# A hybrid backbone layer: the output projection's last token tile and the first SwiGLU products in another order

## The chip, the cores and the metric

The program runs on one core of a Trainium2 chip. The metric is device time in microseconds (us). One execution was also taken by the hardware profiler; all rows below are from it.

## The reference, cut to what matters

One layer over 256 context and 1024 latent tokens of 1024 columns, in float32. A mixer (two groups of heads) gives `y`; after it come an output projection with a gated residual, a modulated RMSNorm, and SwiGLU with a gated residual:

```python
    x = x + g1 * (y[:, CTX_LEN:] @ w_out[layer])
    x = x + g2 * swiglu(modulate(rms_norm(x, norm_ffn_g[layer]), sh2, sc2),
                        w_ffn_in[layer], w_ffn_out[layer])
    return rms_norm(x, final_g)
```

`w_ffn_in` is 1024 x 5632, gate and up halves of 2816 columns each.

## The kernel before

Every float32 product is made of three TensorE passes over operands that were split into a high part (`hi`, the rounded value, written by ScalarE) and a low part (`lo`, the rest, a subtraction on VectorE or GpSimd): hi*hi, hi*lo, lo*hi.

**The projection (op).** The latent tokens are eight tiles of 128 (l = 0 to 7). `wo_half(n)` loads and splits one half (512 columns) of the projection's weights. For a tile, `op_y` turns and splits y, `op_mm(y, n)` makes one half of the output columns (24 matmuls of 128x512) and adds the residual on VectorE (L1139, L1140), and `op_norm` does the rest: it stores x1 to memory, squares it on ScalarE (L1148), takes the reciprocal root, scales the tile in two halves (L1150 VectorE, L1151 ScalarE), turns it in eight transposes (L1158, `x1T`), modulates it (`hf`), and makes the operands of the next stage. The tiles come in pairs, 0, 4, 1, 5, 2, 6, 3, 7, since the next stage is a Winograd-Strassen scheme over two halves of the tokens (tiles 0 to 3, tiles 4 to 7) and two halves of the 1024 inner columns.

**The first SwiGLU matrix (ffn).** The operands of the tokens are seven sets: b11 and b21 (the two halves of columns for tiles 0 to 3), b22, and the differences t1 to t4, each as hi and lo. Operand column l % 4 of a set comes from tile l or l - 4, so t1 to t4 and b22 are complete only after tile 7. For an output block f of 128 columns, `ffn_w` takes the weights raw from `wraw` or from a sum (`ws`, GpSimd, L1250) and splits them (`split`, L314 ScalarE and L315 VectorE); `product(f, i)` is one of seven products of 12 matmuls of 128x512; `combine` reads the bank. Products 1 (a11 x b11) and 2 (a12 x b21) fill the same PSUM bank, and `combine(f, 1)` copies it to `m1` between them (L1285). Products 5, 6, 7, 4 need t1, t2, t3, t4. The first two blocks (f = 0 and 11) are taken together, product by product, in the order 1, 2, 5, 6, 7, 4, 3; the others one at a time. `w_sums` makes sums of the second SwiGLU matrix's weights on GpSimd, in between.

**What sets the order.** The code is written in the order in which a scheduler takes it up; the scheduler may move an instruction ahead of others on its engine, and `tc.issue_after` ties one behind another. On the chip each engine works its list off in order and waits for semaphores. A pool's memory can be used anew once the last reader of what lay there is done: `FW` (raw SwiGLU weights and their splits) takes the place of `WO` (the projection's weights), which is closed after the last tile's second `op_mm`.

At the hand-over from op to ffn the code was:

```python
            op_mm(y, int(l == 7))
            if before:
                op_norm(*before)
            op_mm(y, int(l != 7))
            before = l, y
        close(WO)
        close(OY)
        FW = pool("fw", bufs=2)
...
        for f in (0, FT // 2):
            ffn_load(f)
        banks(**{"f%d" % i: 1 for i in range(8)})
        op_norm(*before, tr=("f3", "f7"))
```

Of the kernel before, what the change touches and what calls it, by code (L numbers as in the profile page):

```python
# [17 lines left out]
P = 128  # L18
# [19 lines left out]
def build(nc, tc, ap, dbg=None, stop=None, marks=None):  # L38
# [122 lines left out]
    try:  # L161
# [15 lines left out]
        ones = const("ones", [P, P])  # L177
# [276 lines left out]
        R2 = pool("r2", bufs=2)  # L454
        ada2 = C.tile([P, 2, KT], F32, tag="ada2", name="ada2")
# [628 lines left out]
        OY = pool("oy", bufs=2, side="right")  # L1084
        WO = pool("wo", side="right")
        S.dma_start(gain, ap["gains"])
        slabs = [X[n][:, i, 3].rearrange("p k t -> p (k t)") for n in X for i in range(2)]

        def wo_half(n):

            hi, lo, raws = [], [], [woraw[k % 2] for k in range(KT)]
            if n == 0:
                raws = [OP.tile([P, 4, P], F32, tag="hf", name="hf", bufs=4).rearrange("p k t -> p (k t)")
                        for _ in range(4)]
                for _ in range(2):
                    x1 = OP.tile([P, D], F32, tag="x1", name="x1", bufs=2)
                    raws += [x1[:, 0:512], x1[:, 512:1024]]
            for k in range(KT):
# [3 lines left out]
                for x, nm in ((hi, "hi"), (lo, "lo")):  # L1102
                    x.append(slabs.pop(0) if n and slabs else
                             WO.tile([P, 512], F32R, tag="wo%s%d%d" % (nm, n, k), name="wo" + nm, bufs=1))
# [9 lines left out]
        def op_y(l):  # L1114
            yhi = OY.tile([P, KT, P], F32R, tag="yhi", name="yhi")
            ylo = OY.tile([P, KT, P], F32R, tag="ylo", name="ylo")
            for half in range(2):
                yt = load(OY, dy[l, :, half * 512:half * 512 + 512], "yt", 3, (P, 512))
# [23 lines left out]
        held = {}  # L1142

        def op_norm(l, y, tr=("pc", "pc")):
# [7 lines left out]
            sl = slice((l % 4) * P, (l % 4 + 1) * P)  # L1152
            for half in range(2):
                pt = bank(tr[half], "x1T")
                hf = OP.tile([P, 4, P], F32, tag="hf", name="hf", bufs=4)
                for i in range(4):
                    k = half * 4 + i
                    T.transpose(pt[:, i * P:(i + 1) * P], x1[:, k * P:(k + 1) * P], ident)  # L1158
                for i in range(4):
                    k = half * 4 + i  # L1160
                    if l % 4 == 3 and i % 2:
# [5 lines left out]
                held[l // 4, half] = hf  # L1167
                e = V if l % 4 == 3 else G

                def part(n, src):  # L1170
# [3 lines left out]
                def diff(n, r, p, q, op=ALU.subtract):  # L1174
                    e.tensor_tensor(r, p, q, op)
                    part(n, r)
# [12 lines left out]

        before = None  # L1190
        pairs = (0, 4, 1, 5, 2, 6, 3, 7)
        nxt = op_y(0)
        for i, l in enumerate(pairs):
            y = nxt
            if l != 7:
                nxt = op_y(pairs[i + 1])
            op_mm(y, int(l == 7))
            if before:
                op_norm(*before)
            op_mm(y, int(l != 7))  # L1200
            before = l, y
        close(WO)
        close(OY)
        FW = pool("fw", bufs=2)
        raws = {}

        last_wfi = [None]
# [380 lines left out]
```

## Time and profile before

| what | value |
|---|---|
| median of 3 runs | 1484.49 us (1481.42 to 1485.3) |
| the profiled execution | 1489.96 us, span of its instructions 1488.2 us |
| granted TensorE clock, mean | 0.976 of full speed |
| TensorE busy | 1403.8 us, 94% of the span |
| projection, 728 to 835 us | TensorE busy 103.83 of 107 us |
| hand-over, 835 to 848 us | TensorE busy 7.45 of 13 us, clock 0.61 |
| first SwiGLU matrix after it, 848 to some 1300 us | TensorE busy nearly throughout |

Busy times of an engine are the sum of its instructions; TensorE's matmuls overlap, so in a dense stretch what counts is the distance from one start to the next. The profiled execution is 5.47 us above the median.

### The profile page before, as it was taken

Reading aid. Unit: us, or ns where it says so; the run is one execution under the profiler, and the core shown is the slowest. Engines: PE = TensorE matmul, PEld = TensorE weight load, DVE = VectorE, ACT = ScalarE, POOL = GpSimd, SP = SyncE. Lnnn points to the kernel's source line nnn. Section 1 sums busy time; section 2 is a strip of 40 time slices with the busy share of each in tenths; the row PEclk is TensorE's granted clock in tenths of the full one; section 3 lists DMA queues with packets and bytes.
Section 4 is the critical chain, followed back from the end, with each engine's and each line's share of the span. In section 5 each row is a group of like instructions: output and inputs, shape, how many; then the busy total and the mean of one; then the engine's idle time right before and its main releaser. Section 6 shows DMA issues by size and latency. Waiting matters only on the chain.

```text
span 1488.2 us, 24210 instructions
## 1 busy us (share of the span) xinstructions
PE 1403.8 (94%) x8919; PEld 1206.0 (81%) x8919; DVE 970.4 (65%) x1934; ACT 606.0 (41%) x1268; POOL 639.4 (43%) x589
## 2 busy tenths in 40 slices
PE   7999999987889999999799899999999999999997
PEld 1898888976878889998688688877888888788886
DVE  6566788378868335778767787656555555657477
ACT  5543564375451111244544433323333333444444
POOL 0120011476124333234326579999555553335321
PEclk9999999997989999999999899999999999999999
DMA  9536686478687745995643256665222232785863
GB/s 324 206 114 203 185 261 200 155 248 252 190 243 199 263 157 203 377 378 202 229 148 110 90 186 231 252 237 198 106 107 107 106 142 74 235 290 184 303 209 114
DMA packets 173751, 298.16 MB, mean 200 GB/s; under 512 B 43368, under 2 KB 93752, under 8 KB 168256
## 3 DMA queue, kind: packets, MB, share of 16 engines
q1 hardware_dynamic: 121760, 252.12, 49.5%
q10 hardware_dynamic: 49072, 35.83, 7.8%
q0 software_dynamic: 2800, 8.65, 1.6%
q8 instruction: 70, 1.15, 0.3%
q14 instruction: 49, 0.40, 0.1%
HBM read 206.60 MB, written 89.96 MB: 199 GB/s over the span
## 4 chain that ended last, share of the span: by engine, by line
PE 46%; DMA 9%; POOL 7%; DVE 4%; issue 3%; ACT 1%; SPq 1%; ACTq 0%; POOLq 0%; DVEq 0%
PE ffn L1279 6%; PE ffn L1277 6%; PE ffn L1278 6%; PE fo L1405 4%; PE fo L1403 4%; PE fo L1404 4%; DMA wd<-tw 2%; PE op L1136 2%; PE op L1138 2%; PE op L1137 2%; PE Tr L884 1%; DMA U<-xd 1%; POOL ws L1250 1%; PE tm L343 1%; POOL tw L1331 1%
## 5 line engine op out<-in xcount | busy, mean ns | idle before, releaser
L341 PE MATMUL tm<-whi,hhi 128*128 128x256 f32 (+1 forms) x704 | 201.0, 289 | 3.5 <-ACT xa L354 1.9
L342 PE MATMUL tm<-wlo,hhi 128*128 128x256 f32 (+1 forms) x704 | 201.9, 288 | 2.1 <-DVE wlo L315 2.1
L343 PE MATMUL tm<-whi,hlo 128*128 128x256 f32 (+1 forms) x704 | 199.8, 287 | 0.0
L341 PEld LDWEIGHTS tm<-whi,hhi 128*128 128x128 f32 x704 | 134.3, 192 | 7.3 <-ACT xa L354 2.5
L1277 PE MATMUL ffn<-t,whi 128*128 128x512 f32 x352 | 137.0, 390 | 1.4 <-ACT whi L314 1.4
L1279 PE MATMUL ffn<-t,wlo 128*128 128x512 f32 x352 | 137.1, 390 | 1.2 <-DVE wlo L315 1.2
L342 PEld LDWEIGHTS tm<-wlo,hhi 128*128 128x128 f32 x704 | 135.2, 192 | 3.4 <-DVE wlo L315 2.7
L1278 PE MATMUL ffn<-t,whi 128*128 128x512 f32 x352 | 137.0, 389 | 0.0
L343 PEld LDWEIGHTS tm<-whi,hlo 128*128 128x128 f32 x704 | 134.6, 192 | 1.8 <-issue 0.9
L314 ACT ACTIVATE whi<-wraw 128x512 fp32r<-128x512 f32 (+2 forms) x98 | 75.2, 771 | 144.0 <-PE ffn L1278 81.9
L314 ACT ACTIVATE whi<-ws 128x512 fp32r<-128x512 f32 x88 | 55.6, 632 | 176.1 <-PE ffn L1278 122.5
L315 DVE TENSOR_TENSOR wlo<-ws,whi 128x512 fp32r<-128x512 f32 x88 | 94.0, 1069 | 45.4 <-ACT whi L314 44.9
L1403 PE MATMUL fo<-whi,ahi 128*128 128x512 f32 x308 | 119.3, 389 | 0.8 <-ACT ahi L314 0.8
L1404 PE MATMUL fo<-wlo,ahi 128*128 128x512 f32 x308 | 119.9, 389 | 0.0
L1405 PE MATMUL fo<-whi,alo 128*128 128x512 f32 x308 | 119.0, 390 | 0.0
L315 DVE TENSOR_TENSOR wlo<-wraw,whi 128x512 fp32r<-128x512 f32 (+2 forms) x92 | 102.9, 1120 | 22.6 <-ACT whi L314 22.2
L1277 PE MATMUL ffn<-b,whi 128*128 128x512 f32 x264 | 104.2, 395 | 3.9 <-ACT whi L314 3.9
L1279 PE MATMUL ffn<-b,wlo 128*128 128x512 f32 x264 | 104.0, 394 | 1.7 <-DVE wlo L315 1.7
L1278 PE MATMUL ffn<-b,whi 128*128 128x512 f32 x264 | 103.9, 394 | 0.0
L576 PE MATMUL b<-hhi,whi 128*128 128x512 f32 (+1 forms) x256 | 96.0, 375 | 1.5 <-ACT y L580 1.5
L578 PE MATMUL b<-hhi,wlo 128*128 128x512 f32 (+1 forms) x256 | 95.0, 371 | 0.0
L577 PE MATMUL b<-hlo,whi 128*128 128x512 f32 (+1 forms) x256 | 94.7, 370 | 0.0
(428 smaller groups left out, 3495.8 us busy)
## 6 DMA issues: line engine op xcount, KB each, us to landing
adaw<-ada_w SPq DMA_DIRECT2D x48, 512.0 KB, 5.2
pk<-sd SPq DMA_DIRECT2D x16, 1536.0 KB, 8.3
wraw<-wfi SPq DMA_DIRECT2D x44, 512.0 KB, 4.0
ar<-ad SPq DMA_DIRECT2D x33, 512.0 KB, 4.8
w<-wfo SPq DMA_DIRECT2D x22, 512.0 KB, 5.5
wd<-tw SPq DMA_DIRECT2D x11, 1024.0 KB, 4.9
ad<-act SPq DMA_DIRECT2D x20, 512.0 KB, 2.8
raw<-wd SPq DMA_DIRECT2D x20, 512.0 KB, 5.5
```

The source lines that it names most:

```text
L314: S.activation(hi, raw, AF.Copy)
L315: e.tensor_tensor(lo, raw, hi.bitcast(F32), ALU.subtract)
L341: T.matmul(o, hhi[:, k, tsl], whi[:, k % 4, :], start=(k == 0), stop=False)
L342: T.matmul(o, hhi[:, k, tsl], wlo[:, k % 4, :], start=False, stop=False)
L343: T.matmul(o, hlo[:, k, tsl], whi[:, k % 4, :], start=False, stop=(k == KT - 1))
L576: T.matmul(o, whi[:, k, :], hh, start=(k == 0), stop=False)
L1277: T.matmul(o, whi[:, k, :], xhi(xn, slice(0, 4), k), start=(first and k == 0), stop=False, **kw)
L1278: T.matmul(o, whi[:, k, :], xlo(xn, slice(0, 4), k), start=False, stop=False, **kw)
L1279: T.matmul(o, wlo[:, k, :], xhi(xn, slice(0, 4), k), start=False, stop=(k == 3), **kw)
L1403: T.matmul(po[g][i], ahi[:, ts], whi, start=(j == 0 and not kw), stop=False, **kw)
L1404: T.matmul(po[g][i], ahi[:, ts], wlo, start=False, stop=False, **kw)
L1405: T.matmul(po[g][i], alo[:, ts], whi, start=False, stop=(j == FH - 1), **kw)
```

## The change

Three things are moved, and some buffers with them.

1. **Weights of the first two blocks.** `WO` now holds only half 0 of the projection's weights, half 1 has pools of its own (`WO1`, operand memory that is not yet in use, one old raw buffer). The last tile runs half 0 first; then `WO` is closed, `early_loads` loads the gate half of the weights of f = 11 and f = 0 and splits a11 and a12 of both, and only then half 1 of the last tile is multiplied.
2. **The last two tiles' norm.** `op_norm` became a generator with three parts. Tile 6's last part (its splits into t1 to t4 and b22) is tied behind the copy of `m1`; tile 7's square is tied behind the last early split, the scaling of its second half behind the copy of `m1`, its transposes behind product 2. Product 5 is made over three token quarters first, and over the fourth when tile 7 is there (`q` in `product`).
3. **Order and engines.** The tiles run 0, 1, 4, 2, 5, 3, 6, 7. The splits of tiles 3, 6 and 7 are on VectorE, those of the others on GpSimd. The operands for tiles 4 to 7 are made from b11 and b21 as hi and lo parts (two subtractions in place of one), with t3 and b22 of tiles 6 and 7 on GpSimd. The four subtractions of `w_sums` stand between products, one by one, instead of after the block. `ones` is loaded later.

The diff, cut:

```diff
-        slabs = [X[n][:, i, 3].rearrange("p k t -> p (k t)") for n in X for i in range(2)]
+        slabs = [X[n][:, i, 3].rearrange("p k t -> p (k t)") for n in ("t1", "t2", "t3", "t4", "b22") for i in range(2)]
...
-                raws = [OP.tile([P, 4, P], F32, tag="hf", name="hf", bufs=4).rearrange("p k t -> p (k t)")
-                        for _ in range(4)]
-                for _ in range(2):
-                    x1 = OP.tile([P, D], F32, tag="x1", name="x1", bufs=2)
-                    raws += [x1[:, 0:512], x1[:, 512:1024]]
+                raws = []
+                for tag in ("x1", "xl"):
+                    for _ in range(2):
+                        x1 = OP.tile([P, D], F32, tag=tag, name=tag, bufs=2)
+                        raws += [x1[:, 0:512], x1[:, 512:1024]]
...
-        def op_norm(l, y, tr=("pc", "pc")):
+        def op_norm(l, y, tr=("pc", "pc"), hold=None, behind=lambda: None, scale_behind=None):
             _, _, xl, x1 = y
             SY.dma_start(dx1[l], x1)
             ssx = OP.tile([P, 1], F32, tag="ssx", name="ssx")
-            S.activation(xl, x1, AF.Square, accum_out=ssx)
+            with tc.issue_after(hold) if hold is not None else nullcontext():
+                S.activation(xl, x1, AF.Square, accum_out=ssx)
             rs = rsqrt_mean(OP, ssx, 1, "r1", D)
             V.tensor_scalar(x1[:, 0:512], x1[:, 0:512], rs, None, ALU.mult)
-            S.activation(x1[:, 512:1024], x1[:, 512:1024], AF.Copy, scale=rs)
+            with tc.issue_after(scale_behind) if scale_behind is not None else nullcontext():
+                S.activation(x1[:, 512:1024], x1[:, 512:1024], AF.Copy, scale=rs)
...
+            yield
+            after, hfs = behind(), []
             for half in range(2):
...
+                with tc.issue_after(after) if after is not None else nullcontext():
+                    for i in range(4):
+                        k = half * 4 + i
+                        T.transpose(pt[:, i * P:(i + 1) * P], x1[:, k * P:(k + 1) * P], ident)
...
-                    if l % 4 == 3 and i % 2:
+                    if l > 3 and i % 2:
...
+            yield
+            for half, hf in enumerate(hfs):
+                A = V if l in (3, 6, 7) else G
...
                 elif half == 0:
-                    held["t1"] = OP.tile([P, 4, P], F32, tag="hs", name="hs", bufs=1)
-                    diff("t1", held["t1"], hf, held[0, 0])
+                    b12 = hf
+                    hi, lo = both("b11")
+                    A.tensor_tensor(t, hf, hi, ALU.subtract)
+                    A.tensor_tensor(t, t, lo, ALU.subtract)
+                    part("t1", t)
                 else:
-                    t1, b21, b12 = held["t1"], held[0, 1], held[1, 0]
-                    diff("t2", t1, hf, t1)
-                    diff("t3", b12, hf, b12)
-                    diff("t4", b21, b21, t1)
-                    part("b22", hf)
+                    A.tensor_tensor(t, hf, t, ALU.subtract)
+                    part("t2", t)
+                    G.tensor_tensor(b12, hf, b12, ALU.subtract)
+                    part("t3", b12, G)
+                    hi, lo = both("b21")
+                    A.tensor_tensor(t, hi, t, ALU.subtract)
+                    A.tensor_tensor(t, t, lo, ALU.add)
+                    part("t4", t)
+                    part("b22", hf, G)
...
+        def early_loads():
+            for f in F1:
+                raws[f] = [raw_tile()]
+                SY.dma_start(raws[f][0], ap["wfi"][f])
+            hold = None
+            for an, c in (("a11", 0), ("a12", 4)):
+                for f in F1:
+                    w2 = w_tile()
+                    hold = S.activation(w2[:, 0], raws[f][0][:, c:c + 4], AF.Copy).ins
+                    V.tensor_tensor(w2[:, 1], raws[f][0][:, c:c + 4], w2[:, 0].bitcast(F32), ALU.subtract)
+                    early[f, an] = w2[:, 0], w2[:, 1]
+            for f in F1[::-1]:
+                raws[f].append(raw_tile())
+                last_wfi[0] = SY.dma_start(raws[f][1], ap["wfi"][FT + f]).ins
+            return hold
...
+            op_mm(y, 0)
+            if l == 7:
+                norm6 = op_norm(*before)
+                for _ in range(2):
+                    next(norm6)
+            elif before:
+                for _ in op_norm(*before):
+                    pass
+            if l == 7:
+                close(WO)
+                FW = pool("fw", bufs=2)
+                last_split = early_loads()
+            op_mm(y, 1)
...
+        ends = []
+        for f in F1:
+            product(f, 1)
+            copied = combine(f, 1)
+        norm7 = op_norm(*before, tr=("f3", "f7"), hold=last_split, behind=lambda: ends[0], scale_behind=copied)
+        next(norm7)
+        with tc.issue_after(copied):
+            for _ in norm6:
+                pass
+        for f in F1[::-1]:
+            ends.insert(0, product(f, 2))
+        for f in ORDER[:2]:
+            product(f, 5, slice(0, 3))
+        for _ in norm7:
+            pass
+        for i in (5, 6, 7, 4, 3):
             for f in ORDER[:2]:
-                product(f, i)
+                product(f, i, slice(3 if i == 5 else 0, 4))
```

Where the change puts instructions at the hand-over, engine by engine.

ScalarE before, from the square of tile 7 (`xl,ssx`) to the first copy of the bank (`m`); `whi` is the high part of a weight block:

```order
L1148 ACTIVATE xl,ssx<-x_9318 128x1024
L314 ACTIVATE whi<-wraw 128x512
L125 ACTIVATE r1s<-ssx,epsb 128x1
L314 ACTIVATE whi<-wraw 128x512 x3
L314 ACTIVATE whi<-ws 128x512 x2
L1151 ACTIVATE x_9318<-x_9318,r1y 128x512
L1285 ACTIVATE m_9599<-ffn 128x512
```

and after (`w` holds high and low part; tile 6's `hf` now stands here):

```order
L1243 ACTIVATE w<-wraw 128x512 x4
L313 ACTIVATE w<-ws 128x512
L1176 ACTIVATE hf<-x1T,ada_1229 128x128 x2
L1154 ACTIVATE xl,ssx<-x_9327 128x1024
L1176 ACTIVATE hf<-x1T,ada_1229 128x128
L125 ACTIVATE r1s<-ssx,epsb 128x1
L1176 ACTIVATE hf<-x1T,ada_1229 128x128
L1345 ACTIVATE m_9557<-ffn 128x512
```

The four weight splits moved ahead of tile 7's square; the copy of the bank stands behind the square in both.

VectorE before, from the first `hf` of tile 7 to the low part of its t1 (`t_8499`):

```order
L1165 TENSOR_SCALAR hf<-x1T,ada_1229 128x128
L315 TENSOR_TENSOR wlo<-ws,whi 128x512
L1165 TENSOR_SCALAR hf<-x1T,ada_1229 128x128 x3
L1175 TENSOR_TENSOR hs<-hf 128x512
L1175 TENSOR_TENSOR hf<-hf 128x512
L315 TENSOR_TENSOR wlo<-ws,whi 128x512
L1172 TENSOR_TENSOR b_8503<-hf,b_8503 128x512
L1172 TENSOR_TENSOR t_8499<-hs,t_8499 128x512
```

and after, from the first `hf` of tile 7 (`last`) to the same result; `hs` is tile 6's, and t_8498 is t2, t_8502 is t4:

```order
L1179 TENSOR_SCALAR last<-x1T,ada_1229 128x128
L314 TENSOR_TENSOR w<-ws,w 128x512 x2
L1189 TENSOR_TENSOR t_8498<-hs,t_8498 128x512
L1179 TENSOR_SCALAR last<-x1T,ada_1229 128x128
L1208 TENSOR_TENSOR hs<-b_8501,hs 128x512
L314 TENSOR_TENSOR w<-ws,w 128x512
L1209 TENSOR_TENSOR hs<-hs,b_8501 128x512
L1199 TENSOR_TENSOR last<-last,b_8497 128x512
L1200 TENSOR_TENSOR last<-last,b_8497 128x512
L1189 TENSOR_TENSOR t_8502<-hs,t_8502 128x512
L1189 TENSOR_TENSOR t_8499<-last,t_8499 128x512
```

Tile 6's t2 and t4, which GpSimd made during the projection before, now stand on VectorE ahead of tile 7's t1.

TensorE before, where tile 7 is turned between products 1 and 2:

```order
L1279 MATMUL ffn<-b_8497,wlo 128x512
L1158 MATMUL x1T<-ident,x_9318 128x128 x8
L1277 MATMUL ffn<-b_8501,whi 128x512
L1278 MATMUL ffn<-b_8501,whi 128x512
L1279 MATMUL ffn<-b_8501,wlo 128x512
```

and after, at the end of product 5 over three quarters (128x384) and its fourth (128x128):

```order
L1336 MATMUL ffn<-t_8499,w 128x384
L1337 MATMUL ffn<-t_8499,w 128x384
L1338 MATMUL ffn<-t_8499,w 128x384
L1172 MATMUL x1T<-ident,x_9327 128x128 x3
L1336 MATMUL ffn<-t_8499,w 128x128 x2
L1337 MATMUL ffn<-t_8499,w 128x128
```

The transposes of tile 7 stand in product 2 and product 5, and the fourth quarter of product 5 behind all of them.

## Rows read from the trace of the kernel before

**Rows 1.** Stretches: span, TensorE busy (x instructions), then the other engines, clock, DMA.
```profile
835.00:848.00 13.00, 7.45 (x18) 5.15 (x17) 12.77 (x17) 8.00 (x17) 11.10 (x8) 0.61 0.27 105
960.00:1060.00 100.00, 97.46 (x424) 78.93 (x424) 59.02 (x66) 30.29 (x52) 89.16 (x61) 1.00 0.61 213
```
**Rows 2.** TensorE from 834 us in time: start, duration, line, instruction, [idle before <- releaser].
```profile
834.92 0.39 PE L1138 MATMUL op<-wohi,ylo 128*128 128x512 f32 x1
839.19 0.80 PE L1277 MATMUL ffn<-b,whi 128*128 128x512 f32 x1 [3.88 <-ACT whi L314]
842.08 0.80 PE L1279 MATMUL ffn<-b,wlo 128*128 128x512 f32 x1 [1.67 <-DVE wlo L315]
843.10 0.63 PE L1278 MATMUL ffn<-b,whi 128*128 128x512 f32 x1
...
847.78 0.39 PE L1277 MATMUL ffn<-b,whi 128*128 128x512 f32 x1
...
849.84 1.03 PE L1158 MATMUL x1T<-ident,x 128*128 128x128 f32 x8
850.63 0.48 PE L1277 MATMUL ffn<-b,whi 128*128 128x512 f32 x1
...
856.18 0.62 PE L1277 MATMUL ffn<-t,whi 128*128 128x512 f32 x2
...
861.62 0.62 PE L1277 MATMUL ffn<-t,whi 128*128 128x512 f32 x2
```
**Rows 3.** ScalarE from 835 us in time, same columns.
```profile
835.76 0.79 ACT L1162 ACTIVATE hf<-x1T,ada 128x128 f32<-128x128 f32 x2
...
837.48 1.05 ACT L1148 ACTIVATE xl<-x 128x1024 f32<-128x1024 f32 x1
838.52 0.62 ACT L314 ACTIVATE whi<-wraw 128x512 fp32r<-128x512 f32 x1
839.04 0.28 ACT L125 ACTIVATE r1s<-ssx,epsb 128x1 f32<-128x1 f32 x1
...
847.52 0.58 ACT L1285 ACTIVATE m<-ffn 128x512 f32<-128x512 f32 x1
```
**Rows 4.** SyncE's load of the weights, and its transfers' times to landing.
```profile
829.69 3.32 SPq L1213 DMA_DIRECT2D wraw<-wfi  x4
DMA to landing us min/median/max: 3.4/3.7/4.0
```
**Rows 5.** VectorE from 835 us in time.
```profile
835.55 0.68 DVE L1139 TENSOR_TENSOR x<-op,g1r 128x512 f32<-128x512 f32 x1
840.33 1.70 DVE L315 TENSOR_TENSOR wlo<-wraw,whi 128x512 fp32r<-128x512 f32 x1
846.59 0.47 DVE L1150 TENSOR_SCALAR x<-x,r1y 128x512 f32<-128x512 f32 x1
850.47 0.41 DVE L1165 TENSOR_SCALAR hf<-x1T,ada 128x128 f32<-128x128 f32 x1 [1.73 <-PE x1T L1158]
854.79 0.69 DVE L1172 TENSOR_TENSOR b<-hf,b 128x512 fp32r<-128x512 f32 x1
855.39 0.68 DVE L1172 TENSOR_TENSOR t<-hs,t 128x512 fp32r<-128x512 f32 x1
```
**Rows 6.** GpSimd from 838 us in time.
```profile
838.05 3.42 POOL L1250 TENSOR_TENSOR ws<-wraw 128x512 f32<-128x512 f32 x2
848.89 1.29 POOL L1250 TENSOR_TENSOR ws<-wraw 128x512 f32<-128x512 f32 x1 [0.69 <-DVE wlo L315]
```
**Rows 7.** VectorE's splits in the ffn stage, 848 to 1300 us: busy us, mean ns.
```profile
L315 DVE TENSOR_TENSOR wlo<-ws,whi 128x512 fp32r<-128x512 f32 x87 | 93.3, 1074 | 45.4 <-ACT whi L314 44.9
```
**Rows 8.** TensorE, 128-column matmuls of the retention in time.
```profile
716.29 0.39 PE L1026 MATMUL ro<-Rf,qk 128*128 128x128 f32 x2
716.51 0.39 PE L1027 MATMUL ro<-Rb,qk 128*128 128x128 f32 x2
```
**Rows 9.** TensorE's wait at the start of the projection.
```profile
732.42 0.50 PE L1136 MATMUL op<-wohi,yhi 128*128 128x512 f32 x1 [2.39 <-ACT yhi L1125]
```

More of the change, by code (lines that the diff above doesn't have):

```diff
@@ L454, in build @@
         R2 = pool("r2", bufs=2)
+        ones = R2.tile([P, P], F32, tag="ones", name="ones", bufs=1)
+        S.dma_start(ones, ap["ones"])
         ada2 = C.tile([P, 2, KT], F32, tag="ada2", name="ada2")
@@ L1102, in wo_half @@
                 for x, nm in ((hi, "hi"), (lo, "lo")):
-                    x.append(slabs.pop(0) if n and slabs else
-                             WO.tile([P, 512], F32R, tag="wo%s%d%d" % (nm, n, k), name="wo" + nm, bufs=1))
+                    if n and slabs:
+                        x.append(slabs.pop(0))
+                    elif n and k == KT - 1 and nm == "hi":
+                        x.append(OR.tile([P, 512], F32R, tag="woraw0", name="wohi"))
+                    else:
+                        x.append((WO1 if n else WO).tile([P, 512], F32R, tag="wo%s%d%d" % (nm, n, k), name="wo" + nm, bufs=1))
                 S.activation(hi[k], raw, AF.Copy, scale=g)
@@ L1117, in op_y @@
             for half in range(2):
-                yt = load(OY, dy[l, :, half * 512:half * 512 + 512], "yt", 3, (P, 512))
+                yt = load(OY, dy[l, :, half * 512:half * 512 + 512], "yt", 2, (P, 512))
                 pt = bank_b("yT")
@@ L1211, in ffn_load @@
             for j in range(2):
-                raw = FW.tile([P, KT, P], F32, tag="wraw", name="wraw", bufs=4)
+                raw = raw_tile()
                 last_wfi[0] = SY.dma_start(raw, ap["wfi"][j * FT + f]).ins
                 raws[f].append(raw)
-        for f in (0, FT // 2):
-            ffn_load(f)
+        def early_loads():
[13 more added lines that the diff above has]
+            return hold
+        tiles = (0, 1, 4, 2, 5, 3, 6, 7)
+        nxt = op_y(0)
+        for i, l in enumerate(tiles):
+            y = nxt
+            if l != 7:
+                nxt = op_y(tiles[i + 1])
+            op_mm(y, 0)
[6 more added lines that the diff above has]
+                    pass
+            if l == 7:
+                close(WO)
+                FW = pool("fw", bufs=2)
+                last_split = early_loads()
+            op_mm(y, 1)
+            before = l, y
+        close(WO1)
+        close(OY)
+        FX = pool("fx", bufs=2)
         banks(**{"f%d" % i: 1 for i in range(8)})
-        op_norm(*before, tr=("f3", "f7"))
-        checkpoint("op")
         FH = FT // 2
@@ L1264, in tmp_of, with product @@
         def tmp_of(tag, bufs=1):
-            return FW.tile([P, 512], F32, tag=tag, name=tag, bufs=bufs)
-        def product(f, i):
+            return FX.tile([P, 512], F32, tag=tag, name=tag, bufs=bufs)
+        def product(f, i, q=slice(0, 4)):
             an, xn, bk = PROD[i]
-            whi, wlo = ffn_w(f, an)
+            whi, wlo = early.pop((f, an)) if (f, an) in early else ffn_w(f, an)
+            if q.stop < 4:
+                early[f, an] = whi, wlo
             first = (f, bk) not in pss
-            if first:
+            if (f, bk) not in pss:
                 pss[f, bk] = bank("f%d" % (f // FH * 4 + "abc".index(bk)), "ffn")
             ps = pss[f, bk]
-            o = ps.rearrange("p (a t) -> p a t", t=P)
+            o = ps.rearrange("p (a t) -> p a t", t=P)[:, q]
             kw = {} if first else {"skip_group_check": True}
             for k in range(4):
-                T.matmul(o, whi[:, k, :], xhi(xn, slice(0, 4), k), start=(first and k == 0), stop=False, **kw)
-                T.matmul(o, whi[:, k, :], xlo(xn, slice(0, 4), k), start=False, stop=False, **kw)
-                T.matmul(o, wlo[:, k, :], xhi(xn, slice(0, 4), k), start=False, stop=(k == 3), **kw)
+                T.matmul(o, whi[:, k, :], xhi(xn, q, k), start=(first and k == 0), stop=False, **kw)
+                T.matmul(o, whi[:, k, :], xlo(xn, q, k), start=False, stop=False, **kw)
+                mm = T.matmul(o, wlo[:, k, :], xhi(xn, q, k), start=False, stop=(k == 3), **kw)
+            return mm.ins
         def combine(f, i):
@@ L1353, in build @@
                 combine(f, i)
-            if n in when:
-                w_sums(when[n])
+                next(ws, None)
+            for _ in ws:
+                pass
         close(FS)
@@ L1391, in build @@
         for j in range(1, 4):
-            slot = [FW.tile([P, 4, P], F32R, tag=tag, name=nm, bufs=5).rearrange("p (o k) t -> p o (k t)", o=1)
-                    for nm, tag in (("whi", "whi"), ("wlo", "wlo"), ("ahi", "whi"), ("alo", "wlo"))]
+            slot = [x[:, i].rearrange("p (o k) t -> p o (k t)", o=1) for x in (w_tile(), w_tile()) for i in range(2)]
             fo_load(1, [j], slot, raw_of(FE, 1), last_wfi[0])
```

72 lines of the change are left out of this document (32 added, 40 removed).

## The prediction, made before the changed kernel ran

> **What bounds the kernel now.** I read the busy times by stretch first. TensorE works almost without a break inside the first SwiGLU stage (97.46 of 100 us); at its entry, from 835 to 848 us, it is busy 7.45 of 13 us at a granted clock of 0.61 [rows 1]. What the change can win in its own place is therefore what is lost there. TensorE's instructions in time show it: the last projection matmul ends at 834.92 + 0.39 = 835.31, the first SwiGLU matmul starts at 839.19 after 3.88 us idle (it waits for ScalarE's high part of the weights), the third waits 1.67 us more for VectorE's low part, and then the matmuls follow each other at (847.78 - 843.10) / 11 = 0.425 us, where they take 0.227 at the full clock ((861.62 - 856.18) / 24) [rows 2]. The clock is at 1.2 GHz there: it fell after the idle time and rose again shortly before 847.78. Products 1, 2 and 5 are 72 matmuls, 16.3 us, with 0.79 for the transposes (849.84 to 850.63) 17.1; product 6 starts at 861.62, 26.3 us after the projection's end. So 9.2 us are lost: 5.55 idle, some 3.65 to the clock.
>
> Why the first weights are late is seen on the other engines. The loads were issued from 829.69 on and land 3.4 to 4.0 us after their issue [rows 4], but on ScalarE the first split stands behind tile 7's square and starts at 838.52 [rows 3]; VectorE runs without a break, and its low part at 840.33 takes 1.70 us [rows 5].
>
> **The change, part by part.** I count from T, the end of the last projection matmul. Tile 6's eight transposes stood inside the projection and now follow it (0.79), so T is 0.79 before the old end, and product 6 breaks even at T + 27.1.
>
> *First weights.* Issued behind tile 6's store of x1, which hangs on VectorE's additions 2 to 5 us after that tile's last matmul (T - 11), they land 4.0 us later, by T - 2 at the latest; one split of 0.62 follows [rows 3]. They are needed at T + 0.79. I cost this at nothing: half 1 of tile 7 covers it; without that cover a late load costs its lateness. Product 1 starts at T + 0.79, and the whole 9.2 us seem to go.
>
> *TensorE's own time.* 0.79 + 5.44 + 5.44 + 0.79 for tile 7's transposes, then product 5 over three quarters, 24 matmuls at a price between three quarters of 0.227 and all of it (4.1 to 5.4; I take 4.1, as the columns stream), then the fourth quarter, 24 of 128 columns at 0.11, which the retention shows for pairs [rows 8]: 2.64. Product 6 could start at T + 19.2, 7.9 us early; cutting product 5 costs 1.3 of the 9.2.
>
> *A wait that comes: product 2.* It fills the bank that product 1 filled, so it waits for the copy `m`. On ScalarE this copy stands behind tile 7's square, and the square waits for VectorE's residual addition, which now has two low parts and two `hf` ahead of it: 0.24 + 0.60 + 1.07 + 0.41 + 1.07 + 0.41 + 1.07 = T + 4.9 (prices below). Square 1.05 and a gap of 0.1, two `hf` 0.8, root 0.28, copy 0.58 [rows 3]: T + 7.7. TensorE wants it at T + 6.2 and stands 1.5 us. Before, this copy ended at 848.1, ahead of product 2, since product 1 ran slowly.
>
> *What is late next: t1 of tile 7.* The fourth quarter of product 5 needs it, and it comes out of VectorE's list. From T to the low part of t1 I count 19 instructions of 512 columns with both inputs in SBUF: two low parts of a12, the residual, the low part of s1, two differences for tile 6's t1, the other s1, tile 6's t1, t2 (2) and t4 (3), two of s2, one of s3, tile 7's t1 (2) and its low part. Nine of these work on tile 6; before, its differences and low parts were on GpSimd, done during the projection. The rest is fixed: start 0.24 and first product with g1r 0.60 [rows 5], six `hf` at 0.41, the scaling 0.47, the one-column instructions some 1.0 together, my estimate: 4.8.
>
> The price p of one of the 19 decides. With GpSimd idle it is 0.60 (854.79 to 855.39), against a busy GpSimd 1.70 (840.33) [rows 5]. Over the whole SwiGLU stage the mean is 1.074 [rows 7]. Behind T GpSimd has 11 instructions in some 25 us: both s1, both s2, both s3, t3's difference, t3 and b22 of tile 6, both s4. They take 1.29 alone and 1.71 against VectorE [rows 6], 14 to 19 us. That is the stage's usual mixture, so I take 1.07: t1 is complete at T + 19 x 1.07 + 4.8 = T + 25.1. TensorE would be there at T + 16.6.
>
> The Trainium skill's page "SBUF — State Buffer", section "Who interferes with whom", says that a VectorE instruction with two SBUF inputs contends with a GpSimd instruction that reads SBUF, over a port pair that one of them holds to the end of its instruction. The 1.70 beside 0.60 agrees. With GpSimd never idle, it would make the sum the last rival's, below.
>
> *Behind it.* The fourth quarter takes 2.5 more from there. Product 6's high part for tile 7 stands on ScalarE behind two weight splits, and these wait for buffers that the fourth quarter frees: 1.3 us after its end (0.62 each). Its low part stands behind two more low parts on VectorE: 1.0. So product 6 is under way at T + 19p + 4.8 + 4.8 = T + 29.9, 2.9 us after break-even.
>
> *Clock.* TensorE is idle some 6 us in front of the fourth quarter. After 3.88 us the clock fell and that cost 3.65 [rows 2]; now part of a slow stretch lies inside the other waits. Between 0 and 3.65 I take 2.
>
> *The rest at nothing.* In the projection's start the raw weights now lie in `xl` buffers, so the loads of y behind `xl` on SyncE wait for their splits. Tile 0's 24 matmuls and the wait of 2.39 that ScalarE causes there anyway cover it [rows 9]; without cover it costs that much again. GpSimd's spread subtractions may win back waits from 960 to 1060 us, where TensorE loses 2.5 of 100 us while GpSimd is 89% busy [rows 1], or move them: -2.5 to +2.5. In the mixer some fill-in matmuls (0.2 to 0.3 us each) change places with scan steps: within 2 us either way. The load of `ones` is moved off the start, where it bounds nothing.
>
> **Sum.** Lost before 9.2; the new hand-over is 2.9 longer than the old, clock 2: +4.9. On the profiled execution's 1489.96 that is 1494.9. It lies 5.5 over the median of 1484.49, so I add to the median: 1489.4, say **1489.5**. In general the change gives 19p - 17.5 us, and the clock.
>
> **Rivals.** 0.3%, 4.45 us, is about what a measurement here can tell from no change.
>
> *It does what it says* (p up to 0.69). For it: VectorE ran at 0.60 from 854.79 on, while GpSimd stood still [rows 5]. At 0.60, t1 is there at T + 16.2, before TensorE; product 6 starts at T + 19.2 + 1.3, so 6.6 us are won: 1477.9. Against it: GpSimd stood still there because TensorE was late and its buffers not free.
>
> *The lists balance* (p 0.69 to 0.95, clock kept): at 0.87, 1483.5. For it: VectorE's prices lie at either end, 0.60 or 1.70, and a tied list may fall into GpSimd's gaps; 0.87 is three instructions at 0.60 for one at 1.70.
>
> *GpSimd blocks throughout* (p over 1.4): at 1.70, t1 is there at T + 37.1, product 6 14.8 late, with the clock 1501. Against it: GpSimd waits for VectorE's splits too.
>
> *The first load is late*, behind tile 6's store: product 1 starts later, but as VectorE's list decides, 1 us of it costs at most 1 us; inside the forecast.
>
> **How the numbers follow.** Forecast (p 0.95 to 1.4, clock lost) 0.50, of it 0.10 below p = 1.05, which is within 0.3%; its own range is 1486 to 1496. Balance 0.28, does what it says 0.14, blocked 0.08. So faster 0.14, same 0.28 + 0.10 = 0.38, slower 0.40 + 0.08 = 0.48. The range leaves out the blocked case and gains beyond p = 0.65: 1479 to 1497.
>
> **What would show it.** Right: no wait before product 1; a wait of product 2 for `m` of 1 to 3 us; one of several us before the 128-column matmuls, released by ScalarE's or VectorE's t1; the clock at 0.5 after it; product 6 about 30 us after the last projection matmul. Wrong: the 128-column matmuls follow at once and product 6 starts near T + 20 (VectorE's mean for the list near 0.6), or the change of time lies in the mixer or after 900 us.

## The result, and the profile after

The changed kernel takes 1489.46 us (median of 7 runs, 1487.88 to 1495.16), the kernel before 1483.89 beside it (7 runs): a ratio of 1.004, interval 1.0025 to 1.0055. The forecast was 1489.5. The total is right; its make-up isn't quite: the hand-over lost about twice what was forecast, and the rest of the program gave some of that back.

The profiled execution of after took 1495.16 us (span 1493.4; TensorE busy 1408.6 us, clock 0.975). TensorE from the last projection matmul on, in time (the view of [rows 2]; start, duration, line, instruction, [idle before <- releaser]):

```profile
832.32 0.40 PE L1144 MATMUL op<-wohi,ylo 128*128 128x512 f32 x1
832.55 1.03 PE L1172 MATMUL x1T<-ident,x 128*128 128x128 f32 x8
833.34 0.49 PE L1336 MATMUL ffn<-b,w 128*128 128x512 f32 x1
...
841.47 0.80 PE L1336 MATMUL ffn<-b,w 128*128 128x512 f32 x1 [2.39 <-ACT m L1345]
842.07 0.63 PE L1337 MATMUL ffn<-b,w 128*128 128x512 f32 x1
...
856.27 0.44 PE L1336 MATMUL ffn<-t,w 128*128 128x128 f32 x2 [2.43 <-ACT t L1188]
857.89 0.33 PE L1337 MATMUL ffn<-t,w 128*128 128x128 f32 x1 [1.18 <-DVE t L1189]
...
858.39 0.39 PE L1338 MATMUL ffn<-t,w 128*128 128x128 f32 x1
858.58 0.41 PE L1336 MATMUL ffn<-t,w 128*128 128x128 f32 x1
...
863.65 1.22 PE L1336 MATMUL ffn<-t,w 128*128 128x512 f32 x2 [1.24 <-ACT t L1188]
866.73 0.77 PE L1337 MATMUL ffn<-t,w 128*128 128x512 f32 x1 [1.86 <-DVE t L1189]
867.29 0.63 PE L1338 MATMUL ffn<-t,w 128*128 128x512 f32 x1
...
871.99 0.43 PE L1338 MATMUL ffn<-t,w 128*128 128x512 f32 x1
```

The wait of 3.88 in front of product 1 is gone: its first matmul follows the transposes at 833.34. In its place stand five shorter waits: 2.39 before product 2, 2.43 and 1.18 at the quarter of product 5, 1.24 and 1.86 at product 6. Between them the clock falls: 0.11 us from one 128-column matmul to the next until 858.39 became 0.21, and product 6's matmuls last 0.63 instead of 0.39 until 871.99. The stretches show the same (the view of [rows 1], first row; same columns):

```profile
832.00:845.00 13.00, 10.61 (x45) 8.36 (x44) 12.46 (x19) 7.66 (x16) 9.69 (x7) 0.87 0.19 78
845.00:857.00 12.00, 9.28 (x51) 8.09 (x49) 11.93 (x13) 5.11 (x10) 8.25 (x5) 1.00 0.08 22
857.00:875.00 18.00, 14.01 (x50) 11.44 (x50) 11.99 (x14) 7.73 (x13) 12.80 (x9) 0.62 0.38 138
```

VectorE (third of the engines) is busy 24.39 of the 25 us up to 857: the hand-over now runs at its pace. Its instructions, and below them GpSimd's (the views of [rows 5, 6]):

```profile
836.43 1.46 DVE L1146 TENSOR_TENSOR x<-x,xl 128x512 f32<-128x512 f32 x1
837.81 1.78 DVE L314 TENSOR_TENSOR w<-ws,w 128x512 fp32r<-128x512 f32 x1
...
852.61 0.68 DVE L1209 TENSOR_TENSOR hs<-hs,b 128x512 f32<-128x512 f32 x1
...
853.92 1.63 DVE L1200 TENSOR_TENSOR last<-last,b 128x512 f32<-128x512 f32 x1
855.48 1.75 DVE L1189 TENSOR_TENSOR t<-hs,t 128x512 fp32r<-128x512 f32 x1
857.16 0.68 DVE L1189 TENSOR_TENSOR t<-last,t 128x512 fp32r<-128x512 f32 x1
...
863.11 1.81 DVE L314 TENSOR_TENSOR w<-wraw,w 128x512 fp32r<-128x512 f32 x1 [1.10 <-ACT w L313]
864.84 1.75 DVE L1189 TENSOR_TENSOR t<-last,t 128x512 fp32r<-128x512 f32 x1
```
```profile
847.66 1.75 POOL L1189 TENSOR_TENSOR b<-hf,b 128x512 fp32r<-128x512 f32 x1
852.76 3.92 POOL L1306 TENSOR_TENSOR ws<-wraw,ws 128x512 f32<-128x512 f32 x2 [3.36 <-DVE w L314]
...
863.10 1.27 POOL L1189 TENSOR_TENSOR b<-hf,b 128x512 fp32r<-128x512 f32 x1
864.33 1.71 POOL L1306 TENSOR_TENSOR ws<-ws,wraw 128x512 f32<-128x512 f32 x1
```

While GpSimd waited (849.41 to 852.76) VectorE's instructions took 0.68; it works again from 852.76 on, and VectorE's instruction of 853.92 took 1.63, the next 1.75. An instruction here starts some 0.08 before the one ahead of it has ended in the record, so 0.68 is the prediction's 0.60 from start to start.

To compare runs I use the **way**: from the start of the last projection matmul to the first matmul of product 3. It needs no total, and totals of single executions carry the chance of the mixer (last section). In after it is 882.48 - 832.32 = 50.2 us, in the profiled execution of before 875.22 - 834.92 = 40.3. In after, e1 to e4, e6 and e12 it holds 0.79 for tile 6's transposes, which stand ahead of it in the others. T is, as in the prediction, the end of the last projection matmul.

### The profile page after: what moved, and what is told of

The parts are those of the page before. It is cut to its first block, busy times and chain, and to the rows that moved or that the text cites. A ratio compares the mean times of both kernels' runs of the same rounds, so it can differ in the third digit from the quotient of the medians.

```text
span 1493.4 us, 24273 instructions
## 1 busy us (share of the span) xinstructions
PE 1408.6 (94%) x8943; PEld 1211.2 (81%) x8943; DVE 976.2 (65%) x1933; ACT 607.9 (41%) x1276; POOL 633.2 (42%) x590
## 5 line engine op out<-in xcount | busy, mean ns | idle before, releaser
L1337 PE MATMUL ffn<-t,w 128*128 128x512 f32 (+2 forms) x360 | 141.6, 393 | 3.0 <-DVE t L1189 3.0
L1336 PE MATMUL ffn<-t,w 128*128 128x512 f32 (+2 forms) x360 | 139.2, 394 | 5.2 <-ACT t L1188 3.7
L1338 PE MATMUL ffn<-t,w 128*128 128x512 f32 (+2 forms) x360 | 140.8, 393 | 0.4 <-DVE w L314 0.4
L314 DVE TENSOR_TENSOR w<-ws,w 128x512 fp32r<-128x512 f32 x88 | 94.8, 1079 | 48.8 <-ACT w L313 45.2
L1482 PE MATMUL fo<-wlo,ahi 128*128 128x512 f32 x296 | 115.2, 389 | 0.0
L1481 PE MATMUL fo<-whi,ahi 128*128 128x512 f32 x296 | 115.2, 389 | 0.0
L1483 PE MATMUL fo<-whi,alo 128*128 128x512 f32 x296 | 114.2, 389 | 0.0
L1336 PE MATMUL ffn<-b,w 128*128 128x512 f32 x264 | 103.8, 393 | 2.4 <-ACT m L1345 2.4
L1337 PE MATMUL ffn<-b,w 128*128 128x512 f32 x264 | 103.3, 391 | 0.0
L1338 PE MATMUL ffn<-b,w 128*128 128x512 f32 x264 | 103.2, 391 | 0.0
L313 ACT ACTIVATE w<-ws 128x512 fp32r<-128x512 f32 x88 | 54.9, 627 | 97.2 <-PE ffn L1338 81.7
L314 DVE TENSOR_TENSOR wlo<-raw,whi 128x512 fp32r<-128x512 f32 x74 | 62.4, 870 | 38.4 <-ACT whi L313 38.3
L587 DVE SCALAR_TENSOR_TENSOR y<-u,cw,y 128x1022 f32<-128x1022 f32 (+3 forms) x80 | 81.1, 1030 | 9.2 <-ACT y L581 9.0
```

Of the source, the lines that this page charges most:

```text
L314: e.tensor_tensor(lo, raw, hi.bitcast(F32), ALU.subtract)
L1336: T.matmul(o, whi[:, k, :], xhi(xn, q, k), start=(first and k == 0), stop=False, **kw)
L1337: T.matmul(o, whi[:, k, :], xlo(xn, q, k), start=False, stop=False, **kw)
L1338: mm = T.matmul(o, wlo[:, k, :], xhi(xn, q, k), start=False, stop=(k == 3), **kw)
L1481: T.matmul(po[g][i], ahi[:, ts], whi, start=(j == 0 and not kw), stop=False, **kw)
L1482: T.matmul(po[g][i], ahi[:, ts], wlo, start=False, stop=False, **kw)
```

## The experiments

| run | way | t1 of tile 7 complete | median us (runs) | ratio to before, interval |
|---|---|---|---|---|
| before / e5 again | 40.3 / 39.9 | T + 20.8 / 20.3 | 1483.9 to 1485.7 | |
| after / e6 again | 50.2 / 49.8 | T + 25.1 / 25.6 | 1489.46 (7) / 1490.75 (6) | 1.004, 1.0025 to 1.0055 / 1.0049, 1.003 to 1.0067 |
| e1 sums left out | 44.2 | T + 20.6 | 1489.32 (12) | 1.003, 1.0016 to 1.0044 |
| e2 t2, t4 on GpSimd | 50.2 | T + 24.4 | 1491.22 (12) | 1.0039, 1.0026 to 1.0052 |
| e3 sums after the block | 50.8 | T + 26.3 | 1492.21 (6) | 1.0044, 1.0029 to 1.0059 |
| e4 products 5 and 6 cut | 47.0 | T + 25.5 | 1494.85 (6) | 1.0058, 1.0038 to 1.0077 |
| e7 old order, early weights | 44.3 | T + 23.9 | 1489.7 (8) | 1.0039, 1.0024 to 1.0054 |
| e8 and product 1 cut | 43.3 | T + 22.5 | 1486.28 (12) | 1.001, 0.9997 to 1.0024 |
| e9 and product 5 cut | 45.4 | T + 24.9 | 1487.61 (12) | 1.0025, 1.001 to 1.004 |
| e10 e9, sums evenly | 47.4 | T + 26.0 | 1487.95 (12) | 1.0014, 1.0003 to 1.0026 |
| e11 before, sums evenly | 39.7 | T + 20.2 | 1485.35 (12) | 1.0003, 0.9991 to 1.0016 |
| e12 t1 first | 51.6 | T + 22.9 | 1492.58 (10) | 1.0043, 1.0027 to 1.0059 |

Each ratio is to runs of before taken beside it (medians 1484.74, 1484.93, 1484.5 and 1485.74 for e1 to e4, e5 to e8, e9 to e11, e12).

**e1: is it GpSimd that sets VectorE's price?** After, with three of the four weight sums of the first two blocks left out; raw parts are split in their place.

```diff
-            if n in rule:
+            if n in rule and (f not in F1 or n == "s1"):
```

> The changed kernel, with GpSimd's sums of weights s2, s3 and s4 left out for the first two blocks (the split takes the raw part instead, so these products multiply other weights); the order of VectorE's and TensorE's instructions stays as it is. My theory (VectorE's list of 19 decides, at a price that GpSimd makes): the mean price of the 19 falls from 1.06 us to 0.65 to 0.85, t1 of tile 7 is complete at T + 17 to T + 21 instead of T + 25.2, product 6 is under way at T + 22 to T + 27 instead of T + 34, and the time falls by 6 to 11 us. Rival (the list is not what is waited for, it is the order of the waits between ScalarE and TensorE): the time falls by less than 2 us, and t1 still comes at T + 24 to T + 26.

VectorE, and under it GpSimd, in the stretch of the list:

```profile
847.14 0.68 DVE L1199 TENSOR_TENSOR last<-last,b 128x512 f32<-128x512 f32 x1
...
849.24 0.69 DVE L1189 TENSOR_TENSOR t<-last,t 128x512 fp32r<-128x512 f32 x1
...
855.72 1.78 DVE L1189 TENSOR_TENSOR t<-last,t 128x512 fp32r<-128x512 f32 x1
```
```profile
841.58 1.77 POOL L1189 TENSOR_TENSOR b<-hf,b 128x512 fp32r<-128x512 f32 x1
851.76 1.79 POOL L1205 TENSOR_TENSOR last<-hf,last 128x512 f32<-128x512 f32 x1 [8.42 <-ACT hf L1176]
```

From 843.35 to 851.76 GpSimd does nothing, and every instruction of VectorE's list that starts there, from 844.41 on, takes 0.67 to 0.69; when it works again, VectorE's take up to 1.78. The 19 durations add up to 16.1 us, in after to 21.3; t1 is there 4.5 us earlier, the way is 6.0 shorter; product 6 is under way at T + 28.3, past the T + 27 that I expected at most, since GpSimd works again by then. That is the prediction's step shown by an experiment: the list decides, and GpSimd sets its price. The time fell by far less than 6: the ratio is 0.001 to 0.002 lower than after's, 1.5 to 3 us, with intervals that overlap. Some 3 us are lost again behind the hand-over: from the first matmul of product 3 to TensorE's last one e1 took 605.1 us, after 602.5 and e6 601.6. Part of that is a wait behind a sum of GpSimd at 996 us (TensorE's row; after waits 1.6 at that place):

```profile
996.50 0.79 PE L1336 MATMUL ffn<-t,w 128*128 128x512 f32 x1 [3.39 <-ACT w L313]
```

**e2: a shorter list.** Tile 6's t2 and t4 go from VectorE to GpSimd: five instructions fewer on the list.

```diff
-                A = V if l in (3, 6, 7) else G
+                A = V if l in (3, 7) or (l == 6 and half == 0) else G
```

> The changed kernel, with tile 6's t2 and t4 made on GpSimd: five instructions less in VectorE's list ahead of tile 7's t1, five more on GpSimd. My theory (the length of VectorE's list decides): 14 instructions at 1.1 to 1.25 us put t1 of tile 7 at T + 20 to T + 22.5, product 6 comes 3 to 6 us earlier, the time falls by 2 to 6 us. Rival (GpSimd is the second limit, and what it gets it gives back by a higher price on VectorE or by late sums s2 and s3): the price goes to 1.4 or more, or product 6 waits for s2, and the time stays within 2 us or rises.

The way is the same, 50.2. The wait for `m` was 3.72 here, product 2 ran slowly behind it, and tile 7's transposes came late, so t1 was ready only at T + 24.4, though the list is shorter. The quarter then ran at full clock, 24 matmuls in some 2.5 us, and this helped nothing: product 6 waited 3.63 and 1.80 in place of 1.24 and 1.86. The 14 that were left on VectorE took 1.2 us each, as expected; what was not expected is that VectorE stood still ahead of t1, 1.08 us for the transposes and 1.23 for ScalarE. The five instructions given to GpSimd bought nothing here.

**e3: do the spread subtractions of `w_sums` matter?** After, with the four subtractions behind the block again.

```diff
                 combine(f, i)
-                next(ws, None)
```

> The changed kernel with the four subtractions of w_sums behind the block again, as before the change; the hand-over is not touched. In the one profile of the change the way from the first product 3 to the end was 1.7 us shorter than before. If the spread subtractions are the reason: 1 to 3 us slower than the change. Rival (that difference is chance, or comes from the order of the tiles): within 1 us.

Way 50.8 and ratio 1.0044: no effect to be seen, neither the loss nor the gain of 2.5 that the prediction bounded.

**e4: cut product 6 too.** Products 5 and 6 over three quarters, both fourth quarters behind them.

```diff
         for f in ORDER[:2]:
             product(f, 5, slice(0, 3))
+        for f in ORDER[:2]:
+            product(f, 6, slice(0, 3))
```

> The changed kernel, with product 6 also made over three token quarters ahead of tile 7's quarter of product 5, so that TensorE has 4.2 us more of work that does not need tile 7. My theory (TensorE only waits for t1, t2 of tile 7, and the wait costs itself and the clock behind it): the wait of 3.6 us ahead of the 128-column matmuls goes to below 1 us, the clock stays at 2.4 GHz in them, and product 7 starts 4 to 7 us earlier; 3 to 7 us faster than the change. Rival (everything behind is tied to VectorE's and GpSimd's lists, so the wait only moves to the quarter of product 6 and to t3): within 2 us.

```profile
838.26 0.80 PE L1336 MATMUL ffn<-b,w 128*128 128x512 f32 x1 [2.69 <-ACT m L1345]
...
858.99 0.69 PE L1336 MATMUL ffn<-t,w 128*128 128x128 f32 x2 [1.49 <-ACT t L1188]
861.65 0.48 PE L1337 MATMUL ffn<-t,w 128*128 128x128 f32 x1 [1.97 <-DVE t L1189]
...
999.01 0.79 PE L1336 MATMUL ffn<-t,w 128*128 128x512 f32 x1 [3.30 <-ACT w L313]
```

Product 5's quarter no longer waits; product 6's does. The way is 3.2 shorter. In the time nothing of this arrives: 1494.85 is over after's medians, with an interval that overlaps theirs. In the profiled execution the 3.2 us are lost again behind the hand-over, as in e1: from the first matmul of product 3 to the last matmul it took 605.2 us (after 602.5, e6 601.6), with a wait of 3.3 at 999 us, where after waits 1.6. Why the median lies higher still, no run shows.

**e5, e6: before and after once more**, unchanged, to see how far the way repeats.

> The kernel before, unchanged, profiled a second time: how far do two executions of one program differ, stage by stage? In the one profile of before the mixer ended (first transposes of y) at 728.99 us, in the five of the changed kernel and its variants at 722.4 to 725.5. If the change made the mixer shorter, it ends here at 727 to 731 again. If that was chance: at 722 to 726. The way from the projection's end to the first product 3 should be 40 us again in either case (39 to 41).

> The changed kernel, unchanged, a second time. The way from the projection's end to the first product 3 took 49.9 us in its first profile and 50.6 in the variant with the old w_sums. If that is what the change costs in every execution: 48.5 to 51 here. If it depends on when the clock falls: off by over 2 us. The median: 1488 to 1491.5.

The way repeats to 0.5 us in both (39.9 and 49.8), though the last projection matmul of after starts 6.6 us earlier in e6 than in the first execution. (Two executions of another hand-over, e9 and e10, differ by 2.0; see there.) The mixer of e5 ended at 730.3 us, where the expectation had put "the change made it shorter"; e11, whose mixer is the same, ended it at 724.7, where it had put chance. So the traces alone leave that open.

**e7: the early weights alone.** Old order of the tiles, old hand-over, product 5 whole, tile 6's splits on GpSimd again.

```diff
-        tiles = (0, 1, 4, 2, 5, 3, 6, 7)
+        tiles = (0, 4, 1, 5, 2, 6, 3, 7)
...
-            product(f, 5, slice(0, 3))
...
-                product(f, i, slice(3 if i == 5 else 0, 4))
+                product(f, i)
```

> The changed kernel with the old order of the tiles (0, 4, 1, 5, 2, 6, 3, 7), its norms whole, and products 2 and 5 uncut: of the change the early weights (and the buffers) remain. Tile 6's differences are made on GpSimd within the projection again, and 14 instructions of 512 columns stand in VectorE's list ahead of tile 7's t1 instead of 19. My theory (that list decides): product 1 waits some 4 us for tile 3's b11, t1 of tile 7 is complete at T + 18 to T + 21, product 6 starts at T + 24 to T + 27, and the time is 3 to 7 us below the change's, within 2 us of before. Rival (the loss lies in the early loads and the moved buffers, not in tile 6): as slow as the change, within 2 us.

```profile
829.18 1.19 PE L1331 MATMUL ffn<-b,w 128*128 128x512 f32 x2 [3.25 <-DVE x L1145]
...
848.85 1.22 PE L1331 MATMUL ffn<-t,w 128*128 128x512 f32 x2 [4.89 <-ACT t L1188]
```

The weights are early, and still nothing is won: product 1 waits 3.25 for VectorE to read the projection's sums out of the bank that it is to fill, then product 5 waits 4.89 for t1. The way is 4.3 longer than the 40.0 that before, e5 and e11 have on average. Of the expectation only product 1's wait came about as forecast: t1 comes at T + 23.9, not by T + 21, and the median is no lower than the change's, as the rival had it. The way is shorter than the change's all the same, and this profile lost it behind the hand-over: 606.0 us from product 3 to the last matmul. That the early loads and the moved buffers are the loss does not fit e8, which has them too.

**e8 to e10: e7, with the products cut where they wait.** e8 puts product 1's last quarter (tile 3's tokens) behind its first three. e9 also runs tile 7's norm behind `m` and cuts product 5, as the change does. e10 is e9 with the second matrix's sums spread evenly.

```diff
+        for q in (slice(0, 3), slice(3, 4)):
+            for f in F1:
+                product(f, 1, q)
```
```diff
-        when = {1 + (j * 18) // FH: j for j in range(FH)}
+        when = {min(1 + 2 * j, 8 + j): j for j in range(FH)}
```

> As the kernel with the old order of the tiles, and product 1 made over three token quarters first and over tile 3's quarter behind them. 12 instructions stand ahead of tile 7's t1. My theory: product 1 starts at T, tile 3's quarter waits below 1.5 us, t1 of tile 7 comes at T + 15.5 to T + 18.5 and product 6 at T + 22 to T + 25; 1 to 4 us faster than before. Rival (GpSimd, which is busy some 90% from 880 to 1000 us, takes it back): the hand-over is as short as this, but the wait of TensorE for a sum at some 1000 us grows above 3 us and the time is within 1 us of before or above.

> The kernel with the old order of the tiles and product 1 cut, with three steps more: product 1's bank is no longer that of the last projection product (its wait of 3.25 us for VectorE ahead of product 1 goes), both copies of the bank stand ahead of tile 7's square on ScalarE, and product 5 is cut too, so that 22 us of products stand behind T that don't need tile 7 (product 1 needs tile 3's quarter). My theory (what TensorE can do without tile 7 against VectorE's list of 12): the first product starts at T + 0.1, t1 of tile 7 comes at T + 19 to T + 23, product 6 starts at T + 24 to T + 26.5 (before: T + 26.5; the kernel with product 1 cut: T + 29.4), and the time is 0 to 4 us below before's. Rival (the lists are late whatever TensorE does): the wait only moves behind product 5, the first product 3 comes over 42 us after T, and the time is no better than with product 1 cut alone (some 1486).

> The same, with the sets of w_sums spread evenly over the first 16 blocks (blocks 1, 3, 5, 7, ... instead of 1, 2, 4, 5, 7, 9, ...), which takes one set (6 us of GpSimd) out of the stretch up to 1000 us. If GpSimd's full queue takes gains back there: the wait for a sum at some 1000 us (1.4 to 3.4 us in the runs so far) goes below 0.5 us, and the time is 1 to 4 us below the kernel without this. Rival (what it takes back is small or only moves to a later block): within 1 us.

TensorE of e8, then of e9:

```profile
831.01 0.66 PE L1331 MATMUL ffn<-b,w 128*128 128x384 f32 x1 [3.25 <-DVE x L1145]
...
850.37 0.48 PE L1332 MATMUL ffn<-t,w 128*128 128x512 f32 x1 [2.08 <-DVE t L1189]
```
```profile
833.78 0.33 PE L1332 MATMUL ffn<-b,w 128*128 128x128 f32 x1 [2.20 <-DVE b L1189]
...
851.24 0.69 PE L1331 MATMUL ffn<-t,w 128*128 128x128 f32 x2 [3.61 <-ACT t L1188]
```

The way of e8 is 1.0 us shorter than e7's; in e9, with product 5 cut as well, it is longer again, since the wait only moves behind the three quarters (3.61) and t1 comes later. Neither t1 nor the time came as early as I expected; e9 went as its rival had it. In e10 the wait around 1000 us falls from 2.1 to 0.3, but one of 1.25 stands at 1291.8, the stretch from product 3 to the last matmul is 601.1 us as in e9, and the median doesn't follow. e10's way is 2.0 longer than e9's though the code of the hand-over is the same: here eight matmuls of product 5 ran at the lower clock (0.52 us each in place of 0.33). So a difference of some 2 us between the ways of two single executions, like the 1.0 above, shows nothing yet. e8 is the best of the variants and can't be told from before.

**e11: before, with the sums spread evenly** (the same edit as e10's, on before).

> The kernel before, with the sets of w_sums spread evenly over the first 16 blocks and nothing else. Its TensorE loses 2.5 us between 960 and 1060 us to waits for sums. If GpSimd's load there is the reason: the waits go, and the time is 1 to 3 us below before's. Rival (they only move): within 1 us of before.

1.0003 with an interval around 1: no gain. TensorE still waits 2.1 us in that stretch for weight splits (2.6 in before).

**e12: t1 first.** The list in another order: tile 6's t1, then tile 7's t1, tile 6's other sets behind it.

```diff
-            for _ in norm6:
-                pass
+            next(norm6)
...
+        next(norm7), next(norm7)
+        with tc.issue_after(held[0]):
+            for _ in norm6:
+                pass
```

> The changed kernel, with tile 7's t1 made ahead of tile 6's t2 and t4: VectorE's list is as long as before up to tile 7's t2, but only 14 instructions of 512 columns stand ahead of its t1 instead of 19. My theory as the runs have left it (what counts is the whole list up to what TensorE needs next): t1 comes at T + 19.5 to T + 22, the wait of 3.6 us ahead of the 128-column matmuls goes below 1.5 us, but product 6 waits for tile 7's t2 and gets under way at T + 30 to T + 34 as in the change; the time is within 2 us of the change's (1488 to 1492). Rival (the wait for t1, with the clock behind it, is the whole cost): product 6 gets under way at T + 24 to T + 28 and the time falls by 4 us or more.

```profile
844.27 0.80 PE L1336 MATMUL ffn<-b,w 128*128 128x512 f32 x1 [6.59 <-ACT m L1345]
...
862.48 1.22 PE L1336 MATMUL ffn<-t,w 128*128 128x512 f32 x2 [3.09 <-ACT t L1188]
866.93 0.77 PE L1337 MATMUL ffn<-t,w 128*128 128x512 f32 x1 [3.23 <-DVE t L1189]
```

The wait at product 5's quarter is gone, since t1 is there at T + 22.9. But two splits now stand ahead of the copy `m` on ScalarE (6.59), and product 6 waits longer. It is under way 35.6 us after T; in after 34.0, in e2 33.8, in e6 34.5, in e3 35.2. In these five the waits lie at different places, and the end is the same within 2 us; only e1, where GpSimd is idle for 8.4 us, gets there at T + 28.3.

## Why the prediction was right, step by step

*First weights at nothing:* right. ScalarE began the last three early splits at 831.26, after 0.69 of waiting for the loads, 2.1 us ahead of product 1, which starts at T + 0.6 without a wait. (The second load landed at T - 1.5, a little later than the T - 2 of the forecast.)

*Product 2's wait for `m`:* right in its mechanism. The residual addition and tile 7's square (836.43, 837.92) stand ahead of the copy, as counted; the wait was 2.39, in the repeat 2.86, forecast 1.5. It costs nothing at the end here, since t1 comes later than TensorE and VectorE did not stand still for tile 7's transposes; in e2, with 3.72, it did.

*19 instructions at 1.07:* right. t1 was complete at 857.84, T + 25.1, as forecast: (25.1 - 4.8) / 19 is 1.07. By their durations, which overlap a little, the 19 last 1.12 each; in e6 and e3 t1 came at T + 25.6 and T + 26.3, so the step is right to about 1 us, and the agreement to 0.1 is luck. (Eight of the 19 work on tile 6, not nine as the prediction says; its sum doesn't use that.) Over the whole stage the split's mean is 1.075 (the view of [rows 7]):

```profile
L314 DVE TENSOR_TENSOR w<-ws,w 128x512 fp32r<-128x512 f32 x86 | 92.3, 1075 | 48.8 <-ACT w L313 45.2 <-issue 2.4
```

So p decided between the forecast and the first three rivals, and e1 shows what it depends on: 0.68 beside an idle GpSimd, 1.78 beside a busy one. What the Trainium skill's page "SBUF — State Buffer" says in "Who interferes with whom", that such an instruction of VectorE and one of GpSimd that reads SBUF exclude each other, agrees with this; that GpSimd would never be idle, on which the blocked rival rested, does not hold: it stood still 3.36 us in the list's midst.

*Behind it, and the clock:* too small, the step that failed. Forecast were product 6 under way at T + 29.9 and 2 us for the clock. Measured: T + 34.0. Of the 4.1 between them, 1.8 is the clock (the fourth quarter took 4.3 instead of 2.5) and 2.2 the two low parts ahead of product 6 (863.11, 864.84): I gave them 1.0 together, but GpSimd was busy and they took 1.81 and 1.75. Then the clock cost another 13 x 0.2, some 2.5 us, up to 871.99: 4.3 in all, beyond the 3.65 that the prediction took as its most. Together the way came out at 50.2 (49.8 and 50.8 in e6 and e3) where the forecast amounts to 40.3 + 0.79 + 4.9 = 46.0.

*The rest at nothing:* wrong, the other way. (At the projection's start it held: ScalarE's wait there is 2.2, against 2.39 in [rows 9].) From the first product 3 to the last matmul of TensorE before took 604.2, 604.1 and (e11) 603.3 us, after 602.5, 601.6 and (e3) 601.4: some 2 us come back. As e3 has the old `w_sums`, the spread subtractions aren't the cause. A net hand-over of 9.5 longer (mean of three ways each, less 0.79) minus 2.0 is 7.5; the medians differ by 5.6. What is left, 1.9 us, lies ahead of the projection, by subtraction: from the first projection matmul to their end the executions of after, e6 and e3 took 766.4, 765.7 and 764.7 us, those of before, e5 and e11 757.5, 757.1 and 758.5. That is 7.9 more on average where the medians differ by 5.6, so the mixer should be some 2 us shorter with the change. The prediction bounded the mixer by 2 us either way and put it at nothing; what shortens it, no run shows. So the total is right because the forecast was low at the hand-over and left out what came back; the sign and the mechanism stand on the experiments, the last 2 us of agreement are luck.

*Why 9.2 us of idle and slow TensorE couldn't be won:* in before, t1 of tile 7 was ready at 856.1, and product 5, which needs it, started at 856.18 without a wait [rows 2, 5]. e5 and e11 show the same to 0.1 us. TensorE's late start hid VectorE's list, and the list left little to win: the longest time that VectorE stood still in it after T is the 1.73 us for tile 7's transposes (850.47 in [rows 5]). So, by my estimate, with the list and its prices as they were an earlier product 1 could have brought t1 forward by some 1.7 of the 9.2 us. In no kernel here was t1 there before T + 20.2, and an earlier product 1 only turned the first wait into a later one (e7: 4.89; e9: 3.61). The change in addition put tile 6's splits on VectorE's list; with the old order and these on GpSimd (e7) the way is 5.1 us shorter (50.2 - 0.79 - 44.3), though the median isn't.

## What to carry to other kernels

Before removing a wait of one engine, look at when the next operand that it needs is complete: if that time coincides with the engine's arrival now, the wait is cover and not loss. Price a list on VectorE by what GpSimd does at that moment, instruction by instruction to the last one that somebody waits for, and not by a mean for the list and the best price for the tail. Where a single execution's total moves by chance, compare the length of the stage itself, and of the stretch behind it: in e1 and e4 some 3 us won at the hand-over were lost again behind it.

## What the runs showed of the hardware

The same VectorE instruction (128x512, both inputs in SBUF) takes 0.67 to 0.69 us beside an idle GpSimd and up to 1.8 beside a busy one, with prices between (1.11 and 1.46 in after), and switches from one instruction to the next with GpSimd's work; GpSimd's takes some 1.3 alone and 1.7 to 1.8 against VectorE.

What a wait of TensorE costs afterwards differs. After 1.20 us (e1, before product 2) the matmuls went on at 0.50 and less; after 2.39 (after) they started at 0.80 and 0.63 each; in e6, after 2.86, the first went at full clock and the fall came 1.5 us later:

```profile
835.38 0.50 PE L1336 MATMUL ffn<-b,w 128*128 128x512 f32 x1 [2.86 <-ACT m L1345]
...
836.87 0.58 PE L1336 MATMUL ffn<-b,w 128*128 128x512 f32 x1
837.25 0.63 PE L1337 MATMUL ffn<-b,w 128*128 128x512 f32 x1
```

The projection's first transposes start anywhere from 724.7 to 730.3 us in three executions whose mixer is the same (before, e5, e11), and from 716.8 to 725.6 in the eleven of the changed kernel and its variants. The first spread alone is as much as the change itself moves, and both profiled executions of before lie some 5.5 us over its median.
